# Layer two's projection forms passed through the tiles of later forms, a product kept elsewhere, and the bias store in eight pieces

## The chip, the core and the metric

The kernel runs on one core of one Trainium2 chip. The metric is the device time of one execution in microseconds (us), taken as the median of several runs. One profiled execution of the kernel before gives the rows below.

## What is computed

Two layers over 512 tokens of width 2048, in fp32. Layer one mixes tokens by forgetting attention with 16 heads of 128, layer two by retention with 8 heads (queries and keys 256 wide, values 512). Each layer has one wide input projection, a SiLU gate on the mixer's output, one output projection and a LayerNorm.

```python
def fox_branch(x, w_in, b_f, q_gain, k_gain, w_out):
    proj = jnp.einsum('bsd,de->bse', x, w_in)      # q, k, v, gate, forget
    ...
    return jnp.einsum('bse,ed->bsd', o * jax.nn.silu(gate), w_out)

def retention_branch(x, w_in, w_out):
    proj = jnp.einsum('bsd,de->bse', x, w_in)      # q, k, v, gate
    ...
    o = group_norm_heads(o)
    y = o * jax.nn.silu(gate)                      # (512, 4096)
    return jnp.einsum('bse,ed->bsd', y, w_out)

for i in range(2):
    y = fox_branch(h, ...) if i % 2 == 0 else retention_branch(h, ...)
    h = layer_norm(ALPHA * h + y, ln_gain[i], ln_bias[i])
```

## The kernel before, in words

**Products.** Every fp32 operand is split into a high part (a copy on ScalarE, ACT, L302) and a low part (a subtraction on VectorE, DVE, L303); one product is three matmuls on TensorE, PE (L307 to L309). The large projections are done by the class `Unit`: a quarter scheme with seven products, p1 to p7, instead of eight. Each product multiplies a block of weights with one *form* of the left operand, a quarter of it or a sum of quarters: p1 uses a11, p2 a12, p3 s4, p4 a22, p5 s1, p6 s2 and p7 s3. A finished product is copied from PSUM by ACT (L412, tiles `p` and `u`) or added by DVE (L457).

**Order.** A planner, the class `Order`, writes out the program in slots of one weight block each (twelve 128x512 matmuls on PE). Around the block of a slot it puts the load of later weight blocks (on the queue of SyncE, SP; `w_raw`, L535 and L538), their splits, and steps of *tasks* that run beside the products: heads, LayerNorm, loads of forms. A task gives the slots that it wants to wait and the DVE and ACT time that it costs; a step that does not fit a slot's budget is put later. Where a tile is needed that a task still holds, `require` turns the planner on without multiplying a block, until the tile is free. Engines take their instructions strictly in that order.

**Layer two's output projection.** Its left operand, y, is 512x4096. The heads of the retention form it (`retain`: group norm L1684 to L1686, then y and its negative `ny`, L1710 and L1711), and GpSimd's queue (POOL) adds the pieces into seven forms in device memory (`give_forms`, L788): y_a... for quarters, y_s... for sums, twice, for heads 0 to 3 and heads 4 to 7. Unit 13 is the last head's value and gate; units 14 and 15 multiply the forms of heads 0 to 3, units 16 and 17 those of heads 4 to 7. The first seven forms are therefore fetched while unit 13 and 14 run, the second seven while units 15 and 16 run. The forms come back by `fetch_form` (L790 to L819): it waits for a free tile (for the first seven the 4-column tiles `y0` and `st`, called `room` in the trace, or `w_raw`; for the second seven the 8-column tiles `g0` and `g1`, `y_raw`), loads into it from SP's queue (L811), and three slots later splits it into the form's own tiles (`HOME`). Only then may the next form take the tile. The value tile `in0` that holds the head's inner products (`inner`) is also the tile in which unit 14 wants to keep p1 (`keep`).

**Layer one.** The same function loads the forms of the fox layer's output projection (L808) and, in the task of core 7, a12 and a22 one after the other. In the fox layer too, `biases` (L1462 to L1467) sends the LayerNorm bias row to all 512 rows of the output from POOL's queue: four transfers of 1 MB. Everything else is added onto these rows at the end.

Of the kernel before, what the change touches and what calls it, by code (L numbers as in the profile page):

```python
# [17 lines left out]
P = 128  # L18
# [61 lines left out]
def dve(n):  # L80
    return 0.067 + n / 960
# [149 lines left out]
def trunk(ctx: ExitStack, tc: tile.TileContext, xq, x, fb_f, columns, wf_in, narrow, wide, ln_g, ln_b, rot, decay,  # L231
# [129 lines left out]
    class Unit:  # L361
# [30 lines left out]
        def keep(self, what, bank):  # L392
            n = self.shape[2]
            if self.wide or what == "u2":
# [3 lines left out]
                if tag == "y0":  # L398
                    self.pair = in_room(0, [P, 2, 2, n])
                    t = self.pair[:, 0]  # L400
                else:
                    t = pool.tile([P, 2, n], F32, name=what, tag=tag)
# [387 lines left out]
    def fetch_form(i, name, tags, at=0, to=8, new=True):  # L790

        step = 8 if tags[0][0] == "g" else 4
        for c in range(at, to, step):
            n = min(step, to - c)
            heads = 4 * i if i else c + n + (0 if name in ("a11", "a21", "s3") else 8)

            is_free = lambda t: free[t] > int(t == "st")
            yield need(until=lambda: given[i > 0] >= heads and any(is_free(t) for t in tags))
            if c == 0 and new:
                new_form(name)  # L800
            tag = next(t for t in tags if is_free(t))
            if tag == "st":
                t = new_raw([P, n, 256])
            else:
                take(tag)
                t = in_room(0, [P, n, 256]) if tag == "y0" else pool.tile([P, n, 256], F32, name="y_raw", tag=tag)
            if i == 0:
                nc.sync.dma_start(t, yf[i][name][:, c:c + n])  # L808
            else:
                for e in range(2):  # L810
                    nc.sync.dma_start(t[:, :, e * P:(e + 1) * P], yf[i][name][:, e, c:c + n])  # L811
            for k in range(0, n, 4):
                m = min(4, n - k)
                yield need(dve=dve(m * 256), act=act(m * 256), wait=0 if k else 3)
                split_form(name, t[:, k:k + m], c + k, c + k + m)
            if tag == "st":
                end_raw(t)
            else:
                give(tag)  # L819

    def fetch_forms(i, names, tags, to=8):
        for n in names:
            yield from fetch_form(i, n, tags, 0, to)

    def fetch_while(i, tags):

        take = lambda *names: lambda: spawn(fetch_forms(i, names, tags))
# [1070 lines left out]
```

## Time and profile before

| | us |
|---|---|
| median of 3 runs (2448.52 to 2450.03) | 2448.59 |
| the profiled execution | 2449.38 |
| its span, first to last instruction | 2447.6 |
| PE busy | 2346.9 |
| DVE busy | 1898.2 |
| ACT busy | 1221.2 |

The span is what the rows below measure. A wait row reads: engine, tile and line that waited, what it waited for, the total, the number of waits and the longest. A timeline row ends with the idle time of the engine ahead of it and what released it. A row of a stretch gives the busy time of each engine, the granted share of TensorE's full clock, and the share of the DMA engines.

### The profile page before, as it was taken

To read this page: it belongs to the slowest core of one execution; us is meant where nothing else is said; L and a number is where in the kernel's file an instruction comes from. 1 tells how busy PE (TensorE), PEld (TensorE's weight loads), DVE (VectorE), ACT (ScalarE), POOL (GpSimd) and SP (SyncE) were. 2 spreads that over 40 slices of the span, in tenths; PEclk is the share of its full clock that TensorE was granted. 3 is DMA by queue.
4 is the path that set the end of the run, shared out by engine and by line. 5 is a ranking of instruction groups with operands and counts; after the bars stand their busy time and mean duration, and the time that the engine had idled before them with its cause. 6 is when DMAs were issued, how large, how long until landed. Compare 5 with 4: busy or idle time off the path is not lost.

```text
span 2447.6 us, 34378 instructions
## 1 busy us (share of the span) xinstructions
PE 2346.9 (96%) x13144; PEld 2032.1 (83%) x13144; DVE 1898.2 (78%) x2506; ACT 1221.2 (50%) x1777; POOL 148.0 (6%) x233
## 2 busy tenths in 40 slices
PE   9999999999998999999999999999999999899995
PEld 8788798898798778878989898989888887687784
DVE  4878778778765556677888888888888888778877
ACT  4546456556544534564454545454545455445433
POOL 0000000000000000000010101010101010010002
PEclk9999999999999999999999999999999999999998
DMA  5455454554554357655675757575757567589678
GB/s 210 137 165 175 165 170 162 173 172 154 182 188 148 128 181 237 213 171 203 205 240 167 227 175 211 176 202 186 223 191 221 183 186 246 173 276 284 208 243 176
DMA packets 184853, 473.27 MB, mean 193 GB/s; under 512 B 17744, under 2 KB 62944, under 8 KB 184176
## 3 DMA queue, kind: packets, MB, share of 16 engines
q1 hardware_dynamic: 161072, 403.41, 49.9%
q0 software_dynamic: 23616, 67.66, 10.6%
q8 instruction: 103, 1.69, 0.3%
q14 instruction: 62, 0.51, 0.1%
HBM read 413.30 MB, written 61.91 MB: 194 GB/s over the span
## 4 chain that ended last, share of the span: by engine, by line
PE 69%; DVE 16%; ACT 5%; DMA 5%; issue 3%; SPq 0%; ACTq 0%; DVEq 0%
PE acc L308 21%; PE acc L307 21%; PE acc L309 20%; DVE w_l L303 6%; DVE w_q L551 3%; ACT w_h L302 3%; DMA w_raw<-in_wide 3%; PE mmp L307 2%; PE mmp L308 2%; PE mmp L309 2%; PE mmp L1168 1%; DVE w_raw L547 1%; DVE a L303 1%; DMA x_raw<-in_xq 1%; PE mmp L1023 1%
## 5 line engine op out<-in xcount | busy, mean ns | idle before, releaser
L307 PE MATMUL acc<-w_h,a 128*128 128x512 f32 (+1 forms) x1616 | 584.0, 361 | 19.5 <-DVE p L457 6.6
L308 PE MATMUL acc<-w_l,a 128*128 128x512 f32 (+1 forms) x1616 | 579.2, 358 | 5.6 <-DVE w_l L303 5.6
L309 PE MATMUL acc<-w_h,a 128*128 128x512 f32 (+1 forms) x1616 | 578.1, 358 | 0.0
L303 DVE TENSOR_TENSOR w_l<-w_raw,w_h 128x1024 fp32r<-128x1024 f32 x337 | 411.9, 1223 | 212.0 <-ACT w_h L302 210.0
L302 ACT ACTIVATE w_h<-w_q 128x1024 fp32r<-128x1024 f32 x344 | 363.5, 1058 | 404.3 <-DVE w_q L551 236.8
L302 ACT ACTIVATE w_h<-w_raw 128x1024 fp32r<-128x1024 f32 x337 | 355.6, 1057 | 381.2 <-PE acc L309 201.3
L307 PE MATMUL acc<-w_h,s 128*128 128x512 f32 (+1 forms) x1344 | 494.5, 368 | 11.0 <-ACT w_h L302 7.4
L308 PE MATMUL acc<-w_l,s 128*128 128x512 f32 (+1 forms) x1344 | 490.0, 365 | 9.7 <-DVE w_l L303 9.7
L303 DVE TENSOR_TENSOR w_l<-w_q,w_h 128x1024 fp32r<-128x1024 f32 x344 | 420.3, 1223 | 99.8 <-ACT w_h L302 93.8
L309 PE MATMUL acc<-w_h,s 128*128 128x512 f32 (+1 forms) x1344 | 487.6, 363 | 0.0
L307 PEld LDWEIGHTS acc<-w_h,a 128*128 128x128 f32 x1616 | 307.5, 190 | 65.3 <-issue 11.7
L308 PEld LDWEIGHTS acc<-w_l,a 128*128 128x128 f32 x1616 | 307.6, 190 | 52.0 <-DVE w_l L303 10.6
L309 PEld LDWEIGHTS acc<-w_h,a 128*128 128x128 f32 x1616 | 307.3, 190 | 44.4
L308 PEld LDWEIGHTS acc<-w_l,s 128*128 128x128 f32 x1344 | 257.0, 191 | 52.8 <-DVE w_l L303 17.0
L307 PEld LDWEIGHTS acc<-w_h,s 128*128 128x128 f32 x1344 | 257.0, 191 | 49.3 <-ACT w_h L302 8.6
L309 PEld LDWEIGHTS acc<-w_h,s 128*128 128x128 f32 x1344 | 256.8, 191 | 39.5
L551 DVE TENSOR_TENSOR w_q<-w_q,w_raw 128x1024 f32<-128x1024 f32 x217 | 264.2, 1220 | 8.2 <-DMA w_raw<-in_wide 5.8
L307 PE MATMUL acc<-a,w_h 128*128 128x256 f32 x464 | 132.3, 285 | 1.2 <-ACT w_h L302 1.2
L309 PE MATMUL acc<-a,w_l 128*128 128x256 f32 x464 | 132.1, 285 | 0.8 <-DVE w_l L303 0.8
L308 PE MATMUL acc<-a,w_h 128*128 128x256 f32 x464 | 132.1, 285 | 0.0
L309 PE MATMUL acc<-s,w_l 128*128 128x256 f32 x448 | 126.7, 283 | 0.0
L308 PE MATMUL acc<-s,w_h 128*128 128x256 f32 x448 | 126.7, 283 | 0.0
(249 smaller groups left out, 2954.7 us busy)
## 6 DMA issues: line engine op xcount, KB each, us to landing
w_raw<-in_wide SPq DMA_DIRECT2D x342, 512.0 KB, 3.6
w_raw<-in_narrow SPq DMA_DIRECT2D x146, 512.0 KB, 3.7
w_q<-in_wide SPq DMA_DIRECT2D x60, 512.0 KB, 4.5
room<-in_wide SPq DMA_DIRECT2D x46, 512.0 KB, 4.3
w_q<-in_narrow SPq DMA_DIRECT2D x26, 512.0 KB, 4.4
y_s<-ny POOLq DMA_DIRECT2D x48, 256.0 KB, 7.4
y_s<-y POOLq DMA_DIRECT2D x40, 256.0 KB, 5.6
room<-in_narrow SPq DMA_DIRECT2D x16, 512.0 KB, 4.7
```

Source lines behind the costliest of these rows:

```text
L302: nc.scalar.activation(h, src, AF.Copy)
L303: nc.vector.tensor_sub(l, src, f32(h))
L307: nc.tensor.matmul(ps, a[0], b[0], start=start, stop=False, skip_group_check=True)
L308: nc.tensor.matmul(ps, a[0], b[1], start=False, stop=False, skip_group_check=True)
L309: nc.tensor.matmul(ps, a[1], b[0], start=False, stop=stop, skip_group_check=True)
L547: nc.vector.tensor_add(self.t, self.t, other)
L551: nc.vector.tensor_add(u.chain[c], u.chain[c], t)
L1023: nc.tensor.transpose(tp[g][:, at], p[q][0][:, k * P:(k + 1) * P], ident)
L1168: nc.tensor.matmul(ps[:, k * P:], vh[:, k], pT[:, k, k * P:], start=k == 0, stop=k == ST - 1)
```

## The change

The forms of layer two's output projection now come in two halves each. A task `loads` runs ahead and puts the raw form into the first tile of a form that is used later (`VIA`: a11 through s1's tile, s1 through s2's, s2 through s4's, s4 through s3's, s3 through a12's, a12 through a22's; a22 goes through `g0`), the halves at least two slots apart. A second task splits each half at least four slots after its load. For the second seven forms this makes 28 transfers of 256 KB of the 14 of 512 KB. Unit 14 keeps p1 in `y0`, which no form passes through any more, instead of `in0`. The bias rows are stored by eight transfers of 512 KB, twelve slots apart, from the start of the third retention head on. In the fox layer the split of a raw form stands four slots behind its load instead of three, and a12 and a22 are fetched side by side.

```diff
@@ -396,7 +396,7 @@
                 require(lambda: free[tag])
                 take(tag)
                 if tag == "y0":
-                    self.pair = in_room(0, [P, 2, 2, n])
+                    self.pair = in_room(0, [P, 1 if self.wide else 2, 2, n])
                     t = self.pair[:, 0]
                 else:
                     t = pool.tile([P, 2, n], F32, name=what, tag=tag)
@@ -787,45 +787,57 @@
             kw = dict(accum_op=ALU.add) if more else {}
             nc.gpsimd.dma_start(yf[i][f][at], y if sign > 0 else ny, **kw)
 
-    def fetch_form(i, name, tags, at=0, to=8, new=True):
-        step = 8 if tags[0][0] == "g" else 4
-        for c in range(at, to, step):
-            n = min(step, to - c)
-            heads = 4 * i if i else c + n + (0 if name in ("a11", "a21", "s3") else 8)
-            is_free = lambda t: free[t] > int(t == "st")
-            yield need(until=lambda: given[i > 0] >= heads and any(is_free(t) for t in tags))
-            if c == 0 and new:
-                new_form(name)
-            tag = next(t for t in tags if is_free(t))
-            if tag == "st":
-                t = new_raw([P, n, 256])
-            else:
-                take(tag)
-                t = in_room(0, [P, n, 256]) if tag == "y0" else pool.tile([P, n, 256], F32, name="y_raw", tag=tag)
-            if i == 0:
-                nc.sync.dma_start(t, yf[i][name][:, c:c + n])
-            else:
-                for e in range(2):
-                    nc.sync.dma_start(t[:, :, e * P:(e + 1) * P], yf[i][name][:, e, c:c + n])
-            for k in range(0, n, 4):
-                m = min(4, n - k)
-                yield need(dve=dve(m * 256), act=act(m * 256), wait=0 if k else 3)
-                split_form(name, t[:, k:k + m], c + k, c + k + m)
-            if tag == "st":
-                end_raw(t)
-            else:
-                give(tag)
-    def fetch_forms(i, names, tags, to=8):
+    def fetch_half(name, c, tags, new):
+
+        heads = c + 4 + (0 if name in ("a11", "a21") else 8)
+        yield need(until=lambda: given[0] >= heads and any(free[t] for t in tags))
+        if new:
+            new_form(name)
+        tag = next(t for t in tags if free[t])
+        take(tag)
+        t = pool.tile([P, 4, 256], F32, name="y_raw", tag=tag)
+        nc.sync.dma_start(t, yf[0][name][:, c:c + 4])
+        yield need(dve=1.14, act=0.97, wait=4)
+        split_form(name, t, c, c + 4)
+        give(tag)
+
+
+    VIA = {"a11": "s1", "s1": "s2", "s2": "s4", "s4": "s3", "s3": "a12", "a12": "a22"}
+    passing = set()
+
+    def fetch_forms(i, names):
+
+        at = {}
+
+        def loads():
+            for n in names:
+                if n not in VIA:
+                    yield need(g0=1)
+                    take("g0")
+                t = pool.tile([P, 8, 256], F32, name="y_raw", tag=home[VIA[n]][0] if n in VIA else "g0")
+                passing.add(VIA.get(n))
+                for c in (0, 4):
+                    yield need(wait=2, until=lambda: given[1] >= 4 * i)
+                    for e in range(2):
+                        nc.sync.dma_start(t[:, c:c + 4, e * P:(e + 1) * P], yf[i][n][:, e, c:c + 4])
+                    at[n, c] = t, o.now
+
+        spawn(loads(), 0)
         for n in names:
-            yield from fetch_form(i, n, tags, 0, to)
-    def fetch_while(i, tags):
-        take = lambda *names: lambda: spawn(fetch_forms(i, names, tags))
-        return {"p5": take("a11", "s1"), "p6": take("s2"), "p7": take("s4", "s3"), "p4": take("a12", "a22")}
+            for c in (0, 4):
+                yield need(dve=1.14, act=0.97,
+                           until=lambda: n not in passing and (n, c) in at and o.now - at[n, c][1] >= 4)
+                if c == 0:
+                    new_form(n)
+                split_form(n, at[n, c][0][:, c:c + 4], c, c + 4)
+            passing.discard(VIA.get(n))
+            if n not in VIA:
+                give("g0")
+
+    def fetch_while(i):
+
+        take = lambda *names: lambda: spawn(fetch_forms(i, names))
+        return {"p5": take("a11"), "p6": take("s1"), "p7": take("s2", "s4"), "p4": take("s3", "a12", "a22")}
 
     def silu_twice(t, tile):
 
@@ -1248,7 +1260,10 @@
         if i in (1, 3, 5):
             vg[(i + 1) // 2].run()
 
-    fetch = lambda *names: lambda: spawn(fetch_forms(0, names, ("k2", "k0", "k1")))
+    def fetch(name, *tags):
+        for c in (0, 4):
+            yield from fetch_half(name, c, tags, c == 0)
+
 
     def other_homes():
 
@@ -1272,7 +1287,7 @@
                     new_form("x21")
                 split_form("x21", t, 4 * c, 4 * c + 4)
                 give(tag)
-            fetch("a11")()
+            spawn(fetch("a11", "k2", "k0", "k1"))
 
         spawn(again(), 1)
 
@@ -1281,12 +1296,9 @@
             new_form(name)
         fox["late"] = True
 
-        def steps():
-            for name in ("a12", "a22"):
-                yield from fetch_form(0, name, ("k0", "k1", "k2"), 0, 4, False)
         core(7)
-        spawn(steps())
+        for name in ("a12", "a22"):
+            spawn(fetch_half(name, 0, ("k0", "k1", "k2"), False))
 
     def two_banks():
         a, b, c = banks
@@ -1294,7 +1306,7 @@
         return a, b
 
     Plain(narrow, 7, pairs[7].take, two_banks, kind="x").run(
-        BOTH, then={len(BOTH) // 2 - 1: fetch("a21"), len(BOTH) - 1: late})
+        BOTH, then={len(BOTH) // 2 - 1: lambda: spawn(fetch("a21", "k2", "k0", "k1")), len(BOTH) - 1: late})
 
 
     zt = {}
@@ -1462,9 +1474,9 @@
     def biases():
 
         nc.gpsimd.dma_start(row_b, ln_b[1:2, :])
-        for s in range(ST):
-            yield need(wait=3)
-            nc.gpsimd.dma_start(out[s * P:(s + 1) * P, :], row_b[0:1, :].to_broadcast([P, D]))
+        for s in range(8):
+            yield need(wait=12)
+            nc.gpsimd.dma_start(out[s * 64:(s + 1) * 64, :], row_b[0:1, :].to_broadcast([64, D]))
 
     def last_banks():
         a, b, c = banks
@@ -1481,7 +1493,6 @@
         return {(0, 0): a, (0, 1): b, (1, 0): c, (1, 1): a}
 
     sink, steps = add_z(1, ALPHA, x_rows, "each")
-    spawn(biases())
     unit = Plain(wide, 5, sink, each_banks)
     unit.run(EACH_N[0], then={0: lambda s=steps: spawn(s(), 1), 15: lambda: spawn(to_columns(0), 1)})
     unit.run(EACH_N[1], then={15: lambda: (there.clear(), spawn(to_columns(1), 1))})
@@ -1747,8 +1758,10 @@
     first.qk_unit.run(EACH[1], then={len(EACH[1]) - 1: lambda: spawn(first.attend())})
     first.vg_unit.run(EACH_N[1], then={len(EACH_N[1]) - 1: lambda: spawn(first.retain())})
     for h in heads[1:]:
+        if h.h == 2:
+            spawn(biases())
         h.qk_unit.run(then={"p3": lambda h=h: spawn(h.attend())})
-        then = fetch_while(1, ("y0", "st")) if h.h == RH - 1 else {}
+        then = fetch_while(1) if h.h == RH - 1 else {}
         last = then.get("p4", lambda: None)
         h.vg_unit.run(leaves=h.h == RH - 1,
                       then={**then, "p4": lambda h=h, last=last: (spawn(h.retain()), last())})
@@ -1772,9 +1785,9 @@
         return sink, steps
 
     sink, steps = add_half(0, 2)
-    Unit(wide, 14, sink, u2="in1", p1="in0").run(then={"p6": lambda s=steps: spawn(s(), 1)})
+    Unit(wide, 14, sink, u2="in1", p1="y0").run(then={"p6": lambda s=steps: spawn(s(), 1)})
     sink, steps = add_half(1, 2)
-    Unit(wide, 15, sink, u2="k2").run(leaves=True, then={0: lambda s=steps: spawn(s(), 1), **fetch_while(2, ("g0", "g1"))})
+    Unit(wide, 15, sink, u2="k2").run(leaves=True, then={0: lambda s=steps: spawn(s(), 1), **fetch_while(2)})
 
     gb = []
```

At the end of unit 13, on ACT: `room` and `y_raw` are raw halves of a11 (and w_h<-room a weight block), `a` is the form's high part, `u` the copy of product p6 out of PSUM, for which PE's next block waits. Before:

```order
L302 ACTIVATE w_h<-w_q 128x1024
L302 ACTIVATE w_h<-w_raw 128x1024
L302 ACTIVATE w_h<-room 128x1024
L302 ACTIVATE a_18634<-room 128x1024
L412 ACTIVATE u_18696<-acc 128x1024
L302 ACTIVATE w_h<-w_raw 128x1024 x3
L302 ACTIVATE inner<-in 128x512
L302 ACTIVATE w_h<-room 128x1024
```

And in the changed kernel:

```order
L302 ACTIVATE w_h<-w_q 128x1024
L302 ACTIVATE w_h<-w_raw 128x1024
L302 ACTIVATE w_h<-room 128x1024
L412 ACTIVATE u_18699<-acc 128x1024
L302 ACTIVATE w_h<-w_raw 128x1024 x2
L302 ACTIVATE a_18757<-y_raw 128x1024
L302 ACTIVATE w_h<-w_raw 128x1024
L302 ACTIVATE inner<-in 128x512
```

The split of a11 stood ahead of the copy `u`; it now stands behind it, and behind two further weight splits.

In unit 14, on PE: `mmp<-v,inner` are the last head's retention matmuls, `acc` the projection's products. Each group of three with one `mmp` needs the group norm of the group before. Before, where they begin, and they go on so for 27 rows:

```order
L307 MATMUL acc<-w_h,a_18634 128x512
L308 MATMUL acc<-w_l,a_18634 128x512
L309 MATMUL acc<-w_h,a_18635 128x512
L307 MATMUL mmp<-v_h,inner 128x512
L308 MATMUL mmp<-v_l,inner 128x512
L309 MATMUL mmp<-v_h,inner 128x512
L307 MATMUL mmp<-v_h,inner 128x512
L308 MATMUL mmp<-v_l,inner 128x512
L309 MATMUL mmp<-v_h,inner 128x512
L307 MATMUL mmp<-v_h,inner 128x512
L308 MATMUL mmp<-v_l,inner 128x512
L309 MATMUL mmp<-v_h,inner 128x512
```

And in the changed kernel:

```order
L307 MATMUL acc<-w_h,s_19047 128x512
L308 MATMUL acc<-w_l,s_19047 128x512
L309 MATMUL acc<-w_h,s_19048 128x512
L307 MATMUL mmp<-v_h,inner 128x512
L308 MATMUL mmp<-v_l,inner 128x512
L309 MATMUL mmp<-v_h,inner 128x512
L307 MATMUL mmp<-v_h,inner 128x512
L308 MATMUL mmp<-v_l,inner 128x512
L309 MATMUL mmp<-v_h,inner 128x512
L307 MATMUL mmp<-v_h,inner 128x512
L308 MATMUL mmp<-v_l,inner 128x512
L309 MATMUL mmp<-v_h,inner 128x512
```

The 27 retention rows, nine triples, stood in one run between blocks of unit 14's first products; now two, three and four triples stand apart, with blocks of twelve product matmuls of p6 between them.

On POOL, the bias row. Before, behind the last gates of the fox layer and ahead of its normalised rows:

```order
L1210 DMA gates_125<-gate 128x1024
L1192 DMA y_a_127<-o 128x256
L1192 DMA y_a_129<-o 128x256
L1464 DMA row_b<-in_ln_b 16x128
L1467 DMA out<-row_b 128x2048 x4
L1406 DMA z_norm_144<-z 128x1024 x2
L1406 DMA z_norm_145<-z 128x1024 x2
L1406 DMA z_norm_146<-z 128x1024 x2
```

And in the changed kernel, in a retention head, where `z_res` is the residual and `y_a`, `y_s` are the forms of y:

```order
L1479 DMA out<-row_b 64x2048 x2
L1750 DMA z_res_149<-z_in 128x512
L1750 DMA z_res_153<-z_in 128x512
L1479 DMA out<-row_b 64x2048
L788 DMA y_a_131<-y 128x512
L788 DMA y_s_132<-y 128x512
L788 DMA y_a_131<-y 128x512
L788 DMA y_s_132<-y 128x512
L1479 DMA out<-row_b 64x2048
```

The four 1 MB transfers in one go became pieces of half the size between the stores of retention heads.

## Rows read from the trace of the kernel before

**Rows 1.** The page: busy time of PE, DVE, ACT and POOL
```profile
PE 2346.9 (96%) x13144; PEld 2032.1 (83%) x13144; DVE 1898.2 (78%) x2506; ACT 1221.2 (50%) x1777; POOL 148.0 (6%) x233
```
**Rows 2.** Waits of PE, 715 to 760 us (waiter <- awaited: total, times, longest)
```profile
PE acc L307 <- ACT x L302: 4.8, 1, 4.8
PE acc L309 <- DVE x L303: 0.5, 1, 0.5
```
**Rows 3.** Waits of ACT, 715 to 760 us
```profile
ACT x L302 <- DMA x_raw<-in_xq: 10.3, 2, 8.1
```
**Rows 4.** DMA issues, 718 to 745 us (KB each, median us to landing)
```profile
out<-row_b POOLq DMA_DIRECT2D x4, 1024.0 KB, 10.5
```
**Rows 5.** Stretches (us; PE, PEld, DVE, ACT, POOL busy (x), PEclk, DMA share, GB/s)
```profile
730.00:735.00 5.00, 5.00 (x43) 4.86 (x41) 0.04 (x1) 0.63 (x1) 0.00 (x0) 1.00 1.01 387
740.00:744.00 4.00, 3.54 (x16) 3.24 (x17) 2.22 (x2) 3.87 (x19) 0.00 (x0) 0.52 0.19 38
744.00:748.00 4.00, 4.00 (x36) 4.00 (x35) 2.71 (x10) 1.75 (x3) 0.00 (x0) 1.00 1.00 375
```
**Rows 6.** Waits of PE, 755 to 860 us
```profile
PE mmp L307 <- ACT qk_h L974: 2.6, 2, 2.1
```
**Rows 7.** Waits of PE in units 13 and 14, 2000 to 2160 us
```profile
PE mmp L307 <- DVE p L1686: 5.0, 1, 5.0
PE acc L307 <- ACT w_h L302: 4.2, 1, 4.2
PE acc L307 <- ACT u L412: 3.6, 1, 3.6
...
PE acc L308 <- DVE w_l L303: 0.5, 1, 0.5
```
**Rows 8.** Timeline of ACT, 2009 to 2028 us (start, us, [idle before <- releaser])
```profile
2024.41 1.06 ACT L302 ACTIVATE a<-room 128x1024 fp32r<-128x1024 f32 x1 [7.32 <-DMA room<-y_a]
2025.38 1.00 ACT L412 ACTIVATE u<-acc 128x1024 f32<-128x1024 f32 x1
```
**Rows 9.** Timeline of ACT, 2126 to 2141 us
```profile
2135.02 1.06 ACT L302 ACTIVATE s<-room 128x1024 fp32r<-128x1024 f32 x1 [6.75 <-DMA room<-y_s]
```
**Rows 10.** Stretches in and behind units 13 and 14
```profile
2026.00:2030.00 4.00, 3.56 (x10) 2.84 (x11) 3.88 (x4) 2.39 (x3) 0.00 (x0) 0.65 0.02 8
...
2098.00:2102.00 4.00, 3.25 (x8) 2.59 (x9) 2.23 (x4) 0.78 (x1) 0.00 (x0) 0.61 0.47 138
...
2138.00:2142.00 4.00, 2.88 (x6) 1.99 (x7) 3.36 (x3) 2.38 (x3) 0.40 (x1) 0.50 1.12 265
```
**Rows 11.** Longer stretches of the same part
```profile
2060.00:2080.00 20.00, 20.00 (x90) 16.57 (x89) 18.57 (x18) 11.20 (x13) 0.57 (x1) 1.00 0.79 268
...
2260.00:2280.00 20.00, 18.35 (x79) 14.19 (x78) 17.18 (x17) 9.99 (x11) 2.67 (x5) 1.00 0.79 256
...
2000.00:2160.00 160.00, 145.74 (x623) 117.29 (x622) 132.06 (x156) 80.85 (x89) 11.47 (x16) 0.96 0.72 220
```
**Rows 12.** Waits of PE in units 15 and 16, 2160 to 2300 us
```profile
PE acc L308 <- DVE w_l L303: 6.7, 8, 2.0
PE acc L307 <- ACT w_h L302: 1.5, 1, 1.5
PE acc L307 <- DVE p L457: 1.3, 1, 1.3
```
**Rows 13.** Waits of ACT, 2160 to 2300 us
```profile
ACT s L302 <- DMA y_raw<-y_s: 6.4, 3, 3.1
ACT ny L1711 <- DMA y_s<-ny: 5.7, 1, 5.7
ACT a L302 <- DMA y_raw<-y_a: 4.4, 2, 3.2
```
**Rows 14.** Timeline of PE, at 2227 us
```profile
2227.07 0.50 PE L308 MATMUL acc<-w_l,s 128*128 128x512 f32 x1 [1.63 <-DVE w_l L303]
```
**Rows 15.** Stretch 1350 to 1400 us, a retention head
```profile
1350.00:1400.00 50.00, 48.71 (x223) 39.83 (x222) 42.31 (x45) 26.92 (x32) 8.45 (x12) 1.00 0.82 237
```

## The prediction, made before the changed kernel ran

> **What bounds the kernel now.** I read the page's busy times first: PE is busy 2346.9 us of a 2447.6 us span, DVE 78%, ACT 50% [rows 1]. So time can only come from PE's gaps and from matmuls that run slowly after them; no arithmetic is removed. Then I read who PE waited for in the three stretches that the order shows as changed (layer one at 715 to 860 us, units 13 and 14 at 2000 to 2160, units 15 and 16 at 2160 to 2300), asked of each releaser what it had itself waited for, and last looked at the granted clock behind each gap. The reader should see that PE's waits name ACT or DVE, while the engine named was waiting for a transfer or working off a backlog.
>
> **Layer one, the bias store.** PE waits 4.8 us for ACT's high part of x and 0.5 us for DVE's low part [rows 2]. ACT had waited up to 8.1 us for the load x_raw [rows 3]. Ahead of it four 1 MB bias transfers land after 10.5 us in the median [rows 4], and with them the DMA engines are full, share 1.01 at 387 GB/s [rows 5]. Behind the gap the granted clock is 0.52 of 2.4 GHz, that is mostly the 1.2 GHz level: 16 matmuls in 3.54 busy us, where the next four us hold 36, nine a us [rows 5]. At nine a us 3.54 us would hold 31.9, so 15.9 are missing, 1.8 us. The change takes the bias out of this stretch: 4.8 + 0.5 + 1.8 = 7.1 us. At its new place a piece is half as large and the next one twelve slots away, and PE still has 48.71 busy us of 50 at a DMA share of 0.82 [rows 15]; I cost it at nothing, with the stall just read, 7.1 us, as the upper bound if one piece holds up a weight load there. Two other edits of layer one, the split four slots behind its load and a12 and a22 side by side, shift steps between attention steps. Nothing here shows which way; the largest wait of the kind is 2.1 us [rows 6], so I take 0, from -2 to +2.
>
> **Unit 13, a11.** PE waits 3.6 us for the copy u [rows 7]. ACT stood 7.32 us at the split of a11 until its load landed, and u came right behind it [rows 8]. In the new order u stands ahead of that split with two weight splits between, and the split four slots behind its load instead of three, so ACT can be late without PE seeing it. Behind the gap the clock is 0.65 and ten matmuls run in 3.56 busy us [rows 10], where 90 in 20 us, 4.5 a us, is usual [rows 11]: 16 - 10 = 6 missing, 1.3 us. Together 4.9 us.
>
> **Unit 14, p1 in y0.** PE waits 5.0 us for DVE's group norm p [rows 7]. That is the planner's jump: p1 needed `in0`, which the retention held, so 27 retention matmuls were put in one run, each group needing a group norm from a DVE that was still behind with weight splits. Afterwards eight matmuls in 3.25 us at clock 0.61 [rows 10]: 14.6 - 8 = 6.6 missing, 1.5 us. With p1 in y0 the triples stand apart as two, three and four, with product blocks between: 6.5 us go. The last four triples still follow each other, and there a shorter wait comes back: between 0 and the whole 5.0 us; I take 1.0, because four triples need about a third of the nine triples' group norms in one go after the first ones are paid beside products.
>
> **Unit 14, s3.** PE waits 4.2 us for ACT's w_h and 0.5 us for w_l [rows 7]; ACT stood 6.75 us at the second half of s3 [rows 9], which was loaded last because its tile came free last. Behind it six matmuls in 2.88 us at clock 0.50 [rows 10]: 13 - 6 = 7 missing, 1.5 us. In the new order the raw of s3 lies in a12's tile many slots earlier: 6.2 us.
>
> **Units 15 and 16.** Two of the eight waits for w_l come from a raw form whose two halves were split at once when it landed: 1.63 us behind s [rows 14], and the longest, 2.0 us, behind a22 [rows 12]; ACT waited 3.1 and 3.2 us for those loads [rows 13]. With halves split four slots after their loads both go, and the DVE backlog behind the first, 1.3 us [rows 12], goes with it: 1.6 + 2.0 + 1.3 = 4.9 us. The 1.5 us behind `ny` [rows 12], where ACT waits 5.7 us for the former piece's stores [rows 13], stays: the last pieces of the retention still stand three slots apart. The other six waits for w_l, 6.7 - 1.6 - 2.0 = 3.1 us, are DVE at its limit and stay, since the number of splits is the same. In units 13 and 14 the gaps that go also gave DVE time to catch up; I put four new waits of half a microsecond there (3.1 / 6), 2.0 us, between 0 and 8 (the first rival).
>
> A transfer in two halves is the place where size matters.
> The Trainium skill, "DMA: Bandwidth & Descriptors", section "Bandwidth", advises transfers of 1 MiB or more, and its section "Anatomy of one DMA" gives about 2.0 us of fixed cost for each, which speaks against this change; as an estimate, 14 further transfers at 2.0 us, if all lay on the path, are 28 us and the time would be 2450, no change. No wait row here separates that cost from the rest, and by the order the transfers run beside other work.
>
> **The sum.** 7.1 + 4.9 + 6.5 + 6.2 + 4.9 = 29.6 us go, 1.0 + 2.0 = 3.0 come back: 26.6 us less. The profiled execution took 2449.4, 0.8 over the median of the runs shown; it would come to 2422.8, the median, 2448.6, to **2422.0**.
>
> **The rivals.**
> *DVE becomes the bound of units 13 and 14.* It is busy 132.06 of 160 us [rows 11]. The forecast shortens this stretch by 17.6 - 3.0 to 145.4 us, a DVE share of 91%. For it: at 86% PE already lost 1.65 of 20 us [rows 11]. Against it: at 93% PE lost nothing [rows 11]. At 86% the stretch is 132.06 / 0.86 = 153.6 us, 8.2 more: 2430. Chance 0.15.
> *A raw load holds SP's queue in unit 15.* The second half of s1 may only be read when the last head's ny has been added; weight loads stand behind it on SP. Against it: weight loads are issued many slots ahead. If it costs one stall like that of s3, 6.2 us: 2428. Chance 0.10.
> *The stall of layer one is not the bias's, or comes back with its pieces.* For it: PE's other waits in that layer have no transfer behind them [rows 6]. Against it: the load landed when the bias did. The 7.1 us stay: 2429. Chance 0.08.
> *The stalls of units 13 and 14 only move*, because the splits still meet loads that have not landed and the jump of the planner comes at another block. 14.6 us of gain are missing, 2437, and if the same happens in units 15 and 16 and the stall of layer one stays as well, 2449, no change. Chance 0.11, of which 0.06 for no change.
> *Slower: each of the 28 halves brings its own stall.* Each half has a split on ACT, ahead of weight splits, and its load has four slots to land. If each of them waits as the raw form of s did, 1.6 us on PE [rows 14], that is 45 us: 2467. It decides from 26.6 / 28 = 0.95 us per half on. Against it: only some of the loads of before were waited for at all [rows 13]. Chance 0.06.
>
> **How the numbers follow.** The forecast has 0.50. Its own lower end is 2422 with nothing coming back (3.0), the 1.5 and 3.1 us of units 15 and 16 gone as well, and 2 us from layer one: 2413. Upwards the range takes in the rivals to 2437, which leaves out the no-change part, the slower one and a little below 2413, under 0.2. A measurement of this kernel can tell about 0.2%, 4.9 us, from no change: faster than that 0.50 + 0.15 + 0.10 + 0.08 + 0.05 = 0.88, within it 0.06, slower 0.06.
>
> **What would show it.** In the changed profile PE must have no wait near 735 us of layer one, and no half-speed stretch there; in unit 13 the copy u must not follow a wait for a transfer; the mmp matmuls of unit 14 must wait less than 2 us for p; no wait of ACT for y_raw may be longer than some 2 us in units 14 to 16; the ny wait must still be there. DVE at over 90% with many waits for w_l would show the first rival; SP issuing weights late in unit 15 the second; an 8 us wait of ACT for x_raw without the bias the third. I am wrong if PE's waits between 2000 and 2300 us sum to more than half of what they were.

## The result, and the profile after

| | before | after |
|---|---|---|
| median, us | 2449.03 | 2409.1 (2407.88 to 2411.64, 4 runs) |
| ratio of the runs | 1 | 0.9851, interval 0.9835 to 0.9868 |
| span of the profiled execution, us | 2447.6 | 2408.0 |

The kernel is 39.9 us faster by the two medians, whose own ratio, 0.9837, lies inside the interval; the interval allows 32 to 40 us. Two executions below stood far outside the others, one of the four of e3 (8418.56 us) and one of the two of e14 (6694.02), so e14 is told by its other run alone. The forecast was 2422 with a range from 2413 to 2437: right in direction, but the time lies 3.9 us below the range. Busy times of the page after, to be laid beside [rows 1]: PE has lost 12 us of busy time, as fewer of its matmuls run at the lower clock (the mean granted clock went from 0.986 to 0.992), and DVE and ACT do what they did.

```profile
PE 2334.7 (97%) x13144; PEld 2023.4 (84%) x13144; DVE 1896.8 (79%) x2506; ACT 1221.5 (51%) x1777; POOL 150.5 (6%) x237
```

**Where the time went.** Both kernels run the same 11712 product matmuls (`acc`) in the same number, so the k-th of one trace can be laid beside the k-th of the other. The difference of the two start times is how far the changed kernel is ahead there; what it grows by in a stretch is what was gained in it. This is worked out from the timelines of PE. How finely it tells can be read from runs of the experiments below whose order is the same in a stretch: they agree with the changed kernel within 0.1 us from 729 to 742, from 750 to 876 and from 2006 to 2138 us, but differ from it by -0.6 to +2.3 us from 2138 to 2281, and by some 2 us elsewhere. So the rows of the bias, of layer one's fetches and of units 13 and 14 tell tenths, the others some 2 us.

| start before / after, us | ahead | gained since the row above | forecast |
|---|---|---|---|
| 730.1 / 729.2 | 0.9 | 0.9 (start of the program) | 0 |
| 750.1 / 741.9 | 8.2 | 7.3 bias | 7.1 |
| 890.8 / 876.4 | 14.3 | 6.2 fetches of layer one | 0 |
| 2020.2 / 2005.8 | 14.4 | 0.0 everything between | 0 |
| 2060.2 / 2040.1 | 20.1 | 5.7 a11 | 4.9 |
| 2170.0 / 2138.3 | 31.8 | 11.6 p1, s3 and what comes back | 9.7 |
| 2320.2 / 2281.2 | 39.0 | 7.3 units 15 and 16 | 4.9 |
| 2400.0 / 2361.1 | 38.9 | -0.1 | 0 |

The stretch of [rows 5] in the changed kernel (us; PE, PEld, DVE, ACT, POOL busy (x), PEclk, DMA share, GB/s): no gap and no slow matmul, 36 of them in the four us that held 16.

```profile
735.00:740.00 5.00, 5.00 (x44) 5.00 (x44) 3.67 (x14) 2.66 (x3) 0.00 (x0) 1.00 0.97 368
740.00:744.00 4.00, 4.00 (x36) 4.00 (x35) 4.00 (x6) 0.23 (x1) 0.00 (x0) 1.00 0.39 123
```

PE's waits in the later part of layer one, 745 to 890 us, which answer to [rows 6]. The first stood in the kernel before too.

```profile
PE acc L307 <- DVE z L1373: 3.1, 1, 3.1
PE acc L307 <- ACT qk_raw L956: 1.6, 1, 1.6
PE mmp L307 <- ACT qk_h L986: 1.0, 2, 0.5
```

ACT at the end of unit 13, which answers to [rows 8]: the copy u ran as soon as PE's product was there, and a11, two splits later, waited 0.96 us for its load where it had waited 7.32.

```profile
2004.41 1.03 ACT L412 ACTIVATE u<-acc 128x1024 f32<-128x1024 f32 x1 [1.67 <-PE acc L309]
2005.33 1.05 ACT L302 ACTIVATE w_h<-w_raw 128x1024 fp32r<-128x1024 f32 x1
2007.18 1.06 ACT L302 ACTIVATE w_h<-w_raw 128x1024 fp32r<-128x1024 f32 x1 [0.80 <-PE acc L309]
2009.21 1.06 ACT L302 ACTIVATE a<-y_raw 128x1024 fp32r<-128x1024 f32 x1 [0.96 <-DMA y_raw<-y_a]
```

PE's waits from 1985 to 2128 us, units 13 and 14, which answer to [rows 7], then from 2128 to 2262, units 15 and 16, which answer to [rows 12]. All four are waits for DVE; none is for ACT.

```profile
PE acc L307 <- DVE p L457: 1.4, 1, 1.4
PE acc L308 <- DVE w_l L303: 1.2, 3, 0.7
...
PE acc L307 <- DVE p L457: 2.1, 1, 2.1
PE acc L308 <- DVE w_l L303: 1.7, 3, 0.7
```

What ACT still waits for a transfer between 1985 and 2330 us (three rows out of its waits): 2.2 us for forms, where [rows 8, 9, 13] held two waits of about 7 us and five more.

```profile
ACT w_h L302 <- DMA w_raw<-in_wide: 6.2, 4, 3.3
...
ACT ny L1722 <- DMA y_s<-ny: 3.2, 1, 3.2
...
ACT a L302 <- DMA y_raw<-y_a: 2.2, 2, 1.2
```

### The profile page after: what moved, and what is told of

Read it like the earlier page. It is cut to its first block, busy times and chain, and to the rows that moved or that the text cites. A ratio compares the mean times of both kernels' runs of the same rounds, so it can differ in the third digit from the quotient of the medians.

```text
span 2408.0 us, 34403 instructions
## 1 busy us (share of the span) xinstructions
PE 2334.7 (97%) x13144; PEld 2023.4 (84%) x13144; DVE 1896.8 (79%) x2506; ACT 1221.5 (51%) x1777; POOL 150.5 (6%) x237
## 4 chain that ended last, share of the span: by engine, by line
PE 71%; DVE 14%; ACT 5%; issue 5%; DMA 4%; POOL 0%; ACTq 0%; DVEq 0%; SPq 0%; POOLq 0%
PE acc L308 21%; PE acc L307 21%; PE acc L309 21%; DVE w_l L303 5%; DMA w_raw<-in_wide 3%; ACT w_h L302 3%; DVE w_q L551 3%; PE mmp L307 2%; PE mmp L308 2%; PE mmp L309 2%; PE mmp L1180 1%; PE mmp L1035 1%; DVE qk_l L987 0%; DVE w_raw L547 0%; DMA y_s<-ny 0%
## 5 line engine op out<-in xcount | busy, mean ns | idle before, releaser
L309 PEld LDWEIGHTS acc<-w_h,s 128*128 128x128 f32 x1344 | 254.0, 189 | 39.3
L307 PEld LDWEIGHTS acc<-w_h,s 128*128 128x128 f32 x1344 | 254.3, 189 | 38.7 <-ACT w_h L302 2.3
```

What stands on the lines that cost most here:

```text
L307: nc.tensor.matmul(ps, a[0], b[0], start=start, stop=False, skip_group_check=True)
L309: nc.tensor.matmul(ps, a[1], b[0], start=False, stop=stop, skip_group_check=True)
```

## The experiments

All times are medians but that of e14; the changed kernel is at 2409.1. Medians of the kernel before lie between 2446.9 and 2449.03 us from batch to batch, so where a few us matter the start times of the same matmuls decide, as in the table above. They come from one profiled execution of each kernel.

### e1: the bias back in layer one

```diff
+    spawn(biases())          # in layer one
-        if h.h == 2:
-            spawn(biases())
```

The loop of `biases` is put back to four transfers of 1 MB as well (not shown).

> The changed kernel with the bias rows stored as before: four 1 MB transfers in layer one. If the stall of layer one belongs to these transfers alone, the load of x lands late again, PE waits about 4.8 + 0.5 us near 735 us and runs at half clock behind it, and 7.3 us of the gain go: about 2416.4. If the load was late for another reason, or the other edits of layer one cover it, no wait comes back: about 2409.

2417.99, and between 700 and 750 us it falls behind the changed kernel by 8.8 us, after that by no more than 0.3 up to 900. PE's waits from 715 to 760 us are those of [rows 2] again:

```profile
PE acc L307 <- ACT x L302: 5.1, 1, 5.1
PE acc L309 <- DVE x L303: 0.5, 1, 0.5
```

So the stall comes from the bias transfers, with every other edit in place. They are asked for three slots apart, but POOL issued all four within 2.1 us, once the row had landed (kernel before; 720.0 to 721.6 us in e1):

```profile
721.05 2.11 POOL L1467 DMA_DIRECT2D out<-row_b  x4 [4.41 <-DMA row_b<-in_ln_b]
```

### e12: the bias at the new place, in four pieces of 1 MB

```diff
-        for s in range(8):
-            yield need(wait=12)
-            nc.gpsimd.dma_start(out[s * 64:(s + 1) * 64, :], ...)
+        for s in range(ST):
+            yield need(wait=3)
+            nc.gpsimd.dma_start(out[s * P:(s + 1) * P, :], ...)
```

> The changed kernel with the bias rows sent as four transfers of 1 MB three slots apart, at the new place in the retention. If only the place mattered (layer one's load of x came right behind them), the time stays: 2408 to 2411. If the pieces mattered, a weight load or a store of the heads near 1230 to 1260 us lands late and PE waits there: 3 to 7 us more, 2412 to 2416.

2409.06, and from 1000 to 2000 us it moves by 0.5 us against the changed kernel; PE has no wait from 1225 to 1320 us in either. So at the new place four pieces cost as little as eight. But POOL issued the four over 43 us there, only the first two together:

```profile
1240.07 1.06 POOL L1479 DMA_DIRECT2D out<-row_b  x2 [8.26 <-DMA row_b<-in_ln_b]
1267.18 0.53 POOL L1479 DMA_DIRECT2D out<-row_b  x1
1282.68 0.53 POOL L1479 DMA_DIRECT2D out<-row_b  x1
```

Whether the place helped or the longer spacing that came with it, these runs do not tell: neither the four in one go at the new place nor spaced pieces in layer one was run.

### e2, e7, e8, e15: the fetches of layer one

```diff
e2: both edits below
e7:
-        yield need(dve=1.14, act=0.97, wait=4)
+        yield need(dve=1.14, act=0.97, wait=3)
e8:
-        for name in ("a12", "a22"):
-            spawn(fetch_half(name, 0, ("k0", "k1", "k2"), False))
+        def steps():
+            for name in ("a12", "a22"):
+                yield from fetch_half(name, 0, ("k0", "k1", "k2"), False)
+        spawn(steps())
e15:
-        yield need(dve=1.14, act=0.97, wait=4)
+        yield need(dve=1.14, act=0.97, wait=6)
```

> The changed kernel with the forms of layer one fetched as before: split three slots behind the load, a12 and a22 one after the other. The traces of before and after show 6.2 us gained between 750 and 890 us, where I had forecast nothing. If these two edits made it, PE's waits for qk_h, qk_raw and qk_l between 750 and 890 us come back (about 7 us instead of 2.5) and the time is about 2415.3. If the gain came with the bias traffic that is gone from that layer, nothing comes back: about 2409.

> The changed kernel with layer one's forms split three slots behind the load again, a12 and a22 still side by side. Of the 5 to 6 us that both edits of layer one are worth: all of it if it is the distance to the load (2415), none if it is the side by side fetch (2409). If what counts is only between which attention steps a split falls, neither undo gives the whole, and the waits that come back are those whose ACT row ahead is a form's split.

> The changed kernel with a12 and a22 of layer one fetched one after the other again, four slots between load and split kept. All of the 5 to 6 us if the side by side fetch makes them (2415), none if the distance to the load does (2409); the wait for qk_l near 825 us, 1.7 us, belongs to a split of a12 that stands between qk steps, so I expect that one to tell.

> The changed kernel with layer one's forms split six slots behind their load instead of four. If the distance to the load matters there, six is no worse than four: 2406 to 2411. If only the place among the attention steps matters, the waits for qk_h, qk_raw and qk_l change in either direction: a sum between 1 and 8 us instead of 2.5, and the time moves with it, 2408 to 2415.

Between 750 and 875 us e2 falls behind the changed kernel by 6.2 us (2414.19), e7 by 4.5 (2411.72), e8 by 0.0 (2412.15, of which none lies in that stretch). e15 gives 2412.11; it has lost 2.5 us against the changed kernel at 875 us, after having been as much as 7.7 behind at 850. PE's waits from 745 to 890 us in e2, which are those of the kernel before:

```profile
PE acc L307 <- DVE z L1376: 3.1, 1, 3.1
PE mmp L307 <- ACT qk_h L986: 2.6, 2, 2.1
PE acc L307 <- ACT qk_raw L956: 1.9, 1, 1.9
PE mmp L995 <- DVE qk_l L987: 1.7, 1, 1.7
PE acc L307 <- ACT acc L961: 0.8, 1, 0.8
```

and in e15, where others have come:

```profile
PE mmp L995 <- DVE qk_raw L977: 1.7, 1, 1.7
PE mmp L995 <- DVE qk_l L987: 1.4, 1, 1.4
PE mmp L307 <- ACT qk_h L986: 0.9, 2, 0.5
```

The reason stands in ACT's timeline at the 2.1 us wait. In e2 a form's split, 1.05 us, and its DVE half stand between two steps of a head's chain, in which ACT's qk_h and DVE's qk_l wait for each other and PE for both (first fence). In the changed kernel the same split comes right behind the last qk_h (second fence).

```profile
755.30 1.05 ACT L302 ACTIVATE a<-y_raw 128x1024 fp32r<-128x1024 f32 x1
756.25 0.46 ACT L986 ACTIVATE qk_h<-mmp,cols 128x256 fp32r<-128x256 f32 x1
758.04 0.47 ACT L986 ACTIVATE qk_h<-mmp,cols 128x256 fp32r<-128x256 f32 x1 [1.33 <-DVE qk_l L987]
```

```profile
756.00 0.47 ACT L986 ACTIVATE qk_h<-mmp,cols 128x256 fp32r<-128x256 f32 x1 [0.58 <-DVE qk_l L987]
756.38 1.05 ACT L302 ACTIVATE a<-y_raw 128x1024 fp32r<-128x1024 f32 x1
```

Neither split waits for its load in these rows, so the distance to the load is not what counts there, and six slots are no better than four. By these rows it is the place of the split among the steps of a chain in which two engines answer each other. The 1.7 us of qk_l come back only with both edits undone: 6.2 us are more than 4.5 and 0.0.

### e3: p1 kept in in0

```diff
-    Unit(wide, 14, sink, u2="in1", p1="y0")
+    Unit(wide, 14, sink, u2="in1", p1="in0")
```

> The changed kernel with unit 14's p1 kept in in0 again. By the forecast's reason the retention of the last head must be pushed through in one run, PE waits about 5 us for the group norm and runs at half clock behind it: 6.5 us lost, about 2415.6. By the rival, the wait of before came from the DVE backlog of the form splits, which now stand elsewhere: PE waits under 1 us there and the time is 2409 to 2411.

2409.66: no loss, and the forecast's reason is right at the spot all the same. The retention is pushed through in one run again, and PE waits nearly as long as in [rows 7]:

```profile
2078.60 0.50 PE L307 MATMUL mmp<-v_h,inner 128*128 128x512 f32 x1 [4.57 <-DVE p L1697]
```

At matmuls that start at 2094.9 us in the changed kernel and 2100.1 in e3, e3 is 4.7 us further behind than at 2000. At 2299.9 the 4.7 us are back, and 0.3 with them. PE's waits of e3 from 2100 to 2262 us show from where: 1.2 us, against 5.4 us of the changed kernel in the same part (3.5 for p, 1.9 for w_l).

```profile
PE acc L308 <- DVE w_l L303: 1.0, 2, 0.7
PE acc L307 <- DVE p L457: 0.2, 1, 0.2
```

The DVE work of the retention is the same in both. Pushed through while PE stands, it makes one long wait; spread between products, it keeps DVE behind (busy 32.86 of the 34 us from 2094 to 2128, against 28.68 of the 32 from 2100 to 2132 in e3) and makes several short ones. Here the two cost the same. What the edit would be worth beside the former fetches, which use `y0` themselves, was not run.

### e4 and e5: the forms of layer two fetched as before

```diff
e4: fetch_form and its fetch_while for both sets of seven, p1 in in0
e5: the same for the second seven alone
-        then={0: lambda s=steps: spawn(s(), 1), **fetch_while(2)})
+        then={0: lambda s=steps: spawn(s(), 1), **old_while(2, ("g0", "g1"))})
```

> The changed kernel with layer two's forms fetched as before through the free small tiles, and p1 in in0 as that needs; layer one and the bias stay changed. By the ledger of the two traces 24.7 us were gained behind 2000 us; if all of it belongs to these edits and nothing is shared with layer one, 2433.8. If part of it came from somewhere else (the bias pieces, other traffic), less: by the forecast's own terms of 4.9 + 6.5 + 6.2 + 4.9 - 3.0 = 19.5 us it would be 2428.6.

> The changed kernel with only the second seven forms (fetched in units 15 and 16) loaded as before: whole 512 KB forms through g0 and g1, one after the other, both halves split at once. The two traces differ by 7.2 us between 2160 and 2330 us of before. If that belongs to these fetches: about 2416. By the forecast's own term, 4.9 us: 2414. If it is a shared gain of DVE's, moved here from unit 14, less than 2 us: under 2411.

e4 gives 2433.32, 24.2 us more: nothing of the gain behind 2000 us is shared with layer one or the bias. e5 gives 2417.08; by the start times it falls behind the changed kernel by 6.2 us between 2190 and 2320 us. Both come near what the table of start times asks for, 24.6 and 7.3 us.

### e6, e9, e10: how far the split stands behind its load

```diff
-                           until=lambda: n not in passing and (n, c) in at and o.now - at[n, c][1] >= 4)
+                           ... >= 1)      e6; >= 2 in e9, >= 6 in e10
```

> The changed kernel with layer two's forms split from one slot behind their load on, instead of four; the tiles they pass through, and the halves, stay. If the distance between load and split is what took the stalls away, ACT waits for y_raw again, with u or w_h behind it, and more than half of the 17 us of units 13 and 14 go: 2418 to 2425. If the early start through the later forms' tiles is what counts, the split merely comes sooner: under 2412.

> The changed kernel with the split two slots behind the load. One slot gave 2450.5, four 2409.1. A slot is about 2.7 us. If a load has to land before ACT comes to the split, two slots (5.4 us) are near the landing times of before (3.7 to 6.7 us in the median), so some splits wait and others don't: 2415 to 2435, with waits of ACT for y_raw of 1 to 4 us. If any slack beyond one slot is enough: under 2412.

> The changed kernel with the split six slots behind the load. If four slots hide every load, two more give nothing: 2407 to 2412, and no wait of ACT for y_raw is left where the changed kernel shows 1.0 and 1.2 us. If the longer hold of a later form's tile delays the forms behind it, the splits crowd towards the products that need them: DVE waits come back, 2413 or more.

| slots between load and split | median, us |
|---|---|
| 1 | 2450.54 |
| 2 | 2430.5 |
| 4 (the changed kernel) | 2409.1 |
| 6 | 2413.38 |

With one slot everything that the whole change gained is lost. With two, one slot fewer than the former fetches had, the profiled execution is still 5.6 us faster than the kernel before between 2000 and 2320 us; three slots through the new tiles were not run. The waits of ACT from 1985 to 2330 us in e6, and one in e9:

```profile
ACT a L302 <- DMA y_raw<-y_a: 45.0, 8, 9.5
...
ACT s L302 <- DMA y_raw<-y_s: 21.8, 6, 5.3
```

```profile
ACT a L302 <- DMA y_raw<-y_a: 25.7, 9, 6.6
```

All 56 transfers of forms in the changed kernel, from issue to landing:

```profile
DMA to landing us min/median/max: 4.0/5.9/11.4
```

A slot is twelve matmuls at 4.5 a us [rows 11], 2.7 us. Two slots, 5.3 us, are less than the median: in e9 ACT waits at 12 of the 28 splits, 9 of `y_a` and 3 of `y_s`, and hands the wait on to the copies and weight splits behind. Four, 10.7 us, nearly reach the longest. With six no wait for y_raw is left, and nothing is gained by it: by the start times e10 loses 2.7 us against the changed kernel between 2000 and 2325, and PE's waits for DVE there come to 7.9 us against 6.4. That is the second of the two outcomes that I had named. My expectation for e6 was too small: I had counted units 13 and 14 alone. Its profiled execution, the slowest of ten at 2457.01, loses 15.6 us between 2000 and 2200 us, as expected, and another 32.7 between 2200 and 2320, where the second seven forms come.

### e11: raw forms in one go

```diff
-                for c in (0, 4):
-                    yield need(wait=2, until=lambda: given[1] >= 4 * i)
-                    for e in range(2):
-                        nc.sync.dma_start(t[:, c:c + 4, e * P:(e + 1) * P], yf[i][n][:, e, c:c + 4])
+                yield need(wait=2, until=lambda: given[1] >= 4 * i)
+                for e in range(2):
+                    nc.sync.dma_start(t[:, :, e * P:(e + 1) * P], yf[i][n][:, e])
```

> The changed kernel with each raw form loaded in one go, two transfers of 512 KB instead of four of 256 KB in pairs; tiles, order of the forms and the distance of four slots stay. If what counts is the distance to the split, the size doesn't matter: 2407 to 2412. If halves land enough sooner to matter, or their fixed cost costs something, the time moves by more than 3 us: over 2413 in the first case, under 2406 in the second.

2416.49, of which 4.9 us lie behind 2000 us by the start times, 4.4 of them between 2200 and 2225. There ACT waits for a weight block, not for a form, and SP's own rows say why (the first row from ACT, then SP's timeline and SP's waits):

```profile
2202.79 1.06 ACT L302 ACTIVATE w_h<-w_raw 128x1024 fp32r<-128x1024 f32 x1 [7.57 <-DMA w_raw<-in_wide]
...
2187.13 8.46 SPq L821 DMA_DIRECT2D y_raw<-y_s  x2
2195.69 0.53 SPq L538 DMA_DIRECT2D w_raw<-in_wide  x1
...
SPq L821 <- DMA y_s<-ny: 5.3, 1, 5.3
```

The whole form s1 may only be read when the last head's ny has been added; its second transfer stood 5.3 us at the head of SP's queue for that store, and the weight load behind it was issued at 2195.69 and landed 7.0 us later. In the changed kernel the second half of s1 holds the queue too, but less long, and PE waits for no weight load:

```profile
2188.07 4.89 SPq L822 DMA_DIRECT2D y_raw<-y_s  x2
```

So the halves are worth something here, through the order of SP's queue and not through the size of a transfer. The profiled execution of e11 is the slowest of four, and the fastest, 2410.55, lies among those of the changed kernel: how much they are worth stays open.

### e13 and e14: more slots in the old scheme

```diff
-                yield need(dve=dve(m * 256), act=act(m * 256), wait=0 if k else 3)
+                yield need(dve=dve(m * 256), act=act(m * 256), wait=0 if k else 4 if i else 3)   # e14: 6
```

> The kernel before with one edit: layer two's raw forms are split four slots behind their load instead of three, still through the free small tiles, one after the other. If the distance alone gives the gain behind 2000 us, it falls by about 20 us, to 2428. If the tiles are needed, since a longer hold of the few free tiles makes the next loads later, it stays within 5 us of before, 2443 to 2453.

> The kernel before with the split six slots behind the load. Distance alone: at least as good as four slots, under 2430. Tiles needed: the last forms come so late that products wait for them and the planner is pushed on; slower than before, 2450 to 2470.

e13: 2447.99 against 2448.0 of the kernel before, ratio 1.0002 (0.9992 to 1.0013). e14: 2459.81. PE's longest waits from 1985 to 2360 us in e13, and the longest of e14:

```profile
PE acc L307 <- ACT w_h L302: 15.6, 2, 9.7
PE mmp L1706 <- ACT gate L1719: 3.3, 1, 3.3
```

```profile
2172.68 0.76 PE L307 MATMUL acc<-w_h,a 128*128 128x512 f32 x1 [12.78 <-DVE p L457]
```

At a11 the added slot helps: by 2050 us e13 has gained 5.5 us on the kernel before. By 2150 us it stands 9.7 us worse than at 2000, and only behind that it wins some back, 2.1 us in all by 2325. The longest wait has this ahead of it on ACT:

```profile
2134.83 0.60 ACT L1710 ACTIVATE y<-mmp 128x512 f32<-128x512 f32 x1 [5.08 <-DMA y_a<-y]
2140.87 0.60 ACT L1711 ACTIVATE ny<-mmp 128x512 f32<-128x512 f32 x1 [5.44 <-DMA y_s<-ny]
2142.97 1.06 ACT L302 ACTIVATE s<-room 128x1024 fp32r<-128x1024 f32 x1 [1.50 <-DMA room<-y_s]
```

Two steps of the retention, put close behind the former ones, and then the half of a form that came last. That they stand there because each form now holds one of the few small tiles a slot longer, so that the next load starts later and the planner is pushed on, I take from the planner's rule. The last load of the first seven forms does start 15 product matmuls later than in the kernel before (10620 instead of 10605 ahead of it); that this is the reason, no row shows. What the two runs show is that the distance by itself gives nothing in the old scheme. By e9 and e6 the tiles by themselves give little: 5.6 us at two slots, nothing at one.

## Why the prediction was right or wrong

**The bias, right.** 7.1 forecast, 7.3 measured, and e1 returns it. That the new place costs nothing is right, and e12 shows that eight pieces were not needed for it; place and spacing are not told apart. The third rival is out.

**Layer one's fetches, wrong: the largest miss.** The step that failed is "Nothing here shows which way; ... so I take 0, from -2 to +2". It was 6.2 us. The profile did show it: of the waits of [rows 6] with their neighbours, two, 2.1 us for qk_h and 1.7 us for qk_l, had a form's split in the same chain a step or two ahead of the late one, on an engine whose order the change prints row by row. I had the names of the waits and the order of both kernels, but asked only what ACT had waited for, a transfer or a backlog, and not which rows stood ahead of the late one and whether they moved. My bound, one wait more or less, was also too narrow for a stretch with five waits, 7 us, that could all go or come.

**a11, right.** 4.9 forecast, 5.7 measured, by the order that was shown: u ahead of the split.

**p1 in y0, right at its place and worth nothing.** The wait of 5.0 us and the slow matmuls went, and e3 brings them back; but without them DVE stays behind and PE waits 6.4 us in eight short waits from 1985 to 2330 us, where e3 has 5.8 us in all, and e3 is no slower. So the 6.5 us were a term of the sum that the change did not earn; that the sum came as near as it did is in part luck. The forecast had room for it, 1.0 at the last triples, where nothing came back, and 2.0 of new DVE waits; units 13 and 14 show waits for DVE of 1.4 + 1.2 us, close to that. What I did not see is that they belong to this edit and pay all of it back once the waits of units 15 and 16 are counted too.

**s3, and the sum of units 13 and 14.** 9.7 were forecast for p1, s3 and what comes back, 11.6 came. Part is in the short waits for p at L1719 and L457 of the trace before, 0.4 and 0.6 us, that I had not listed. The first rival, DVE as the bound, did not come as I priced it: DVE runs at 132.62 of 143 us, 93%, while PE is busy 140.34.

```profile
1985.00:2128.00 143.00, 140.34 (x618) 113.60 (x618) 132.62 (x158) 77.72 (x83) 9.13 (x13) 1.00 0.79 242
```

**Units 15 and 16, too small.** 4.9 forecast, 7.3 measured. The step that failed is "The 1.5 us behind `ny` ... stays". ACT still waits for the former stores, 3.2 us instead of 5.7, but PE no longer waits for ACT there: the step stands 47 product matmuls later in PE's order, and the w_h behind it is done before PE comes to it. The waits for w_l, of which I let 3.1 us stay as DVE at its limit, fell to 1.7 us (0.8 of the 3.1 had stood right behind the wait for that w_h), and one of 2.1 us for p came. The second rival did not come in the time, as no weight load in that part made PE wait; its mechanism was there, SP's queue standing 4.9 us at the second half of s1, and e11 shows it at a price, 4.4 us.

**The slower rival had its mechanism, not its case.** "Each of the 28 halves brings its own stall" is near what e6 does: at one slot ACT waits at 14 of them, and it costs the whole gain, 41.4 us. Its point of decision, whether four slots hide a landing, could have been had from the trace before: loads into `room` and `y_raw` there were waited for after three. I took the distance of four as hiding them without asking by how much three had missed.

Of the miss of 12.3 us by the start times (38.9 gained, 26.6 forecast), 6.2 are layer one's fetches, 2.4 units 15 and 16, 1.9 unit 14, 0.8 a11, 0.2 the bias, and 0.9 lie ahead of any changed instruction. The lower end of the range, by its own terms, is 2412.4 and not 2413; that alone would not have reached the time.

## What to carry to other kernels

A load that feeds a split on an in-order engine wants a distance that covers its longest landing, not its median, and that distance can only be had if the tile that it lands in is not needed by the next load: here more distance in the old tiles gave nothing, and the new tiles at less distance gave 5.6 of 24.6 us or none. In e11 a load that waited for a store held the loads behind it in its queue. When an order moves, look at every wait of the stretch for the rows just ahead of the late step, above all in chains where two engines answer each other; PE waited 2.1 us behind a single split of one us there, and 0.4 with the split at the end of the chain. And a stall that is removed may only have been where a backlog was paid off: undo the edit by itself before it is credited.

## What the runs showed of the hardware

The bias transfers, 4 MB issued from POOL's queue within 2.1 us, delayed a 512 KB load issued behind them on SP's queue: x_raw landed after 14.6 us and the next one after 4.6, and without the bias in that layer they landed after 4.6 and 4.7. The same 4 MB issued over 43 us cost PE nothing in a stretch with transfers all around (e12, DMA share 0.84 from 1225 to 1300 us). A load that waited for a store held SP's queue for 5.3 us in e11, and the weight load behind it was issued only then. Behind the gaps of PE of 3.6 to 5.0 us the granted clock fell, to 0.50 to 0.65 over four us in [rows 5, 10] and to 0.64 in 2078 to 2082 us of e3, that is mostly 1.2 of 2.4 GHz; in e3 it was back at 0.94 in the next four us.

```profile
2078.00:2082.00 4.00, 3.40 (x9) 2.71 (x10) 3.93 (x6) 0.00 (x0) 0.00 (x0) 0.64 0.81 266
2082.00:2086.00 4.00, 4.00 (x17) 3.26 (x17) 3.87 (x6) 2.92 (x3) 0.00 (x0) 0.94 0.00 0
```

The Trainium skill's advice of transfers of 1 MiB or more ("DMA: Bandwidth & Descriptors", section "Bandwidth") did not decide here: whole forms in two transfers of 512 KB gave 2416.49 us, halves in transfers of 256 KB 2409.1. The rows of e11 put 4.4 us of that on a load that held SP's queue, not on the size of a transfer; forms in transfers of 1 MiB were not run. The 28 us estimated for 14 further transfers, if all lay on the path, did not come: the time fell by 39.9 us.
